# RWKV-7 projections on one Trainium2 core: TensorE in a written order, with tiles of their own for the keys' squares and the decay rows

## The chip, the cores and the metric

The kernel runs on one core of one Trainium2 chip. The metric is the time of one execution on the device, in microseconds (us); several executions are taken and their median stands for the kernel. A profile is one further execution, recorded instruction by instruction.

The engines are called by the names of the profile: PE (TensorE, matmuls), ACT (ScalarE), DVE (VectorE), POOL (GpSimd), and SP (SyncE), which in this kernel issues every data transfer (DMA).

## The reference, cut to what matters

The reference is an encoder trunk of two layers over 512 tokens of width 1024. Each layer is half an FFN, a token mixer, and half an FFN, with layer norms between them. The mixer of the first layer is neighbourhood attention, that of the second is RWKV-7. The change lies in the projections of the RWKV-7 mixer:

```python
xx = 0.5 * (x_prev + x_next) - x
xr, xw, xk, xv, xa, xg = (x + xx * mix[i] for i in range(6))
r = xr @ w_rkv[0];  k = xk @ w_rkv[1];  v = xv @ w_rkv[2]
wl = w0 + tanh(xw @ w1) @ w2            # for both directions z
decay = exp(-exp(-softplus(-wl) - 0.5))
a = sigmoid(a0 + (xa @ a1) @ a2)
g = sigmoid(xg @ g1) @ g2
kk = k * k_k;  kk = kk / max(norm(kk over each head's 64 channels), 1e-12)
```

A recurrent scan over the tokens in both directions follows; it reads all of these.

## The kernel before, in words

Everything is fp32. Where a product needs it, an operand is split into a high and a low part of a reduced type, by ACT (L220, the copy of the high part) and by DVE or POOL (L221, the difference), and a product takes three matmul passes (`mm3`, L225 to L227).

The kernel is written in a language that plans the order of the instructions itself. Its planner walks the program by an estimate of its own of how long everything takes, and puts onto each engine's queue the instruction that was traced earliest among those that are ready. A buffer of a tile pool is handed out when the first instruction that touches the tile is planned. On the chip each engine then runs its queue in that order. A block `manual_schedule(engines=...)` takes the engines named in it out of this: they get their instructions in the order of the program text. `behind(ins)` puts what is traced in its block behind `ins` on the engine of `ins`.

The stage in question is `rwkv_project` (from L570 on). On entry x lies as 8 chunks of 128 channels by 512 tokens (`xraw`). The stage works as follows, in the order of the text:

- `first(2)` (L607 to L623) makes `xx` and the split input `mk` of the keys, chunk by chunk; `mixed(i)` (L593 to L599) makes the split input of another projection: per chunk one DVE instruction at L603 into a tile of the tag `tmp`, one ACT copy (L220), one DVE difference (L221). `mw = mixed(1)` is the decay's input, `ma = mixed(4)` that of a, `mg = mixed(5)` that of the gate. `mg` takes the buffers of `mk`.
- The keys (L648 to L654): 8 input chunks by 8 output chunks into 8 PSUM banks `acc`. These are all the banks there are.
- `raws(3, dram["xv"])` (L631 to L637, called at L657) writes the values' unsplit input to DRAM: per chunk one DVE instruction (L635) into a `tmp` tile and one DMA of 256 KB. The values are computed in the scan, later.
- For each output chunk the bank is copied out by ACT (`store`, L626 to L629: an ACT copy into a quarter of one buffer `evs`, and a DMA), and its square goes by ACT (L661) into a `tmp` tile. A bank is free when both have read it. Eight products with the `heads` matrix (L664) sum the squares of each head into `ss`; two DVE instructions (L666, L667) invert them.
- The decay's first product `pw` (L670, weights w1) and its Tanh; a DMA brings the two halves of 64 rows to `tmp` tiles with a row of ones (L673 to L677), which are split into `wh`.
- `raws(0, dram["xr"])` and the product of its chunks with one column block of the receptance weights, `pr` (L679, L680).
- The product with a1 (L685), `mg`, the decay's second product (L687 to L698: 2 directions by 4 token blocks by 2 halves, each one `mm3`, an ACT Tanh at L696, a DVE instruction at L697 and a DMA), the gate's two first products (L705 to L707), its sigmoid (L711 to L713), and the gate's second product (L714 to L720).

The tag `tmp` has 4 buffers of 128x512. The larger buffers, of 128x2048, that hold `xx`, `evs`, `wh`, `gh`, `mw` and part of `ma` are of the tag `ring`, of which there are 11. Weights go through a `raw` tile and the tag `w`, of 3 buffers. A DMA, too, has its place in one queue, that of SP.

PE's order in this stage is the planner's.

Of the kernel before, what the change touches and what calls it, by code (L numbers as in the profile page):

```python
# [18 lines left out]
P = 128  # L19
# [79 lines left out]
class Trunk:  # L99
# [470 lines left out]
    def rwkv_project(self, dram, xraw, w_rkv, w1, w2, a1, g1, g2, heads):  # L570

        nc = self.nc
        with self.pool("rwa") as pool:
# [10 lines left out]
            evs, ev = quarters(), [0]  # L584
# [4 lines left out]
            def evac():  # L589
                ev[0] += 1  # L590
                return evs[:, ev[0] % 4, :]
# [39 lines left out]
            def raws(i, dst):  # L631

                for c in range(ND):
                    t = self.tmp()
                    nc.vector.scalar_tensor_tensor(t, xx[c], self.col(C_MIX + i, c), xraw[:, c, 1 : S + 1], ALU.mult, ALU.add)  # L635
                    nc.sync.dma_start(dst[:, c, :], t)
                    yield c, t  # L637
# [10 lines left out]
            acc = [self.bank() for _ in range(ND)]  # L648
            for c in range(ND):
                with self.behind(*marks):  # L650
                    u = k_units[c] if c < LEAD else self.load_rows(w_rkv[1], c * P)
                for o in range(ND):
                    self.mm3(halves_of(acc[o]), u[:, 0, o * P : (o + 1) * P], u[:, 1, o * P : (o + 1) * P],
                             *mk.get(c), c == 0, c == ND - 1)  # L654
            ma = mixed(4)

            list(raws(3, dram["xv"]))  # L657
            for o in range(ND):
                store(dram["rkv"][1][:, o, :], acc[o])
                sq = self.tmp()  # L660
                nc.scalar.activation(sq, acc[o], AF.Square, scale=self.col(C_KK, o))  # L661
                if o == 0:
                    ss = self.bank()[:HEADS]
                nc.tensor.matmul(ss, heads_t[:, o, :], sq, start=o == 0, stop=o == ND - 1)  # L664
            iv = evac()[:HEADS]
            nc.vector.tensor_scalar(iv, ss, 1e-24, None, ALU.max)  # L666
            nc.vector.reciprocal(iv, iv)  # L667
            nc.sync.dma_start(dram["iv"], iv)

            pw = self.proj_cols(self.load_cols(w1, 0), mw)  # L670
            wt = evac()
            nc.scalar.activation(wt, pw, AF.Tanh)
# [5 lines left out]
            pr = self.bank()  # L678
            for c, t in raws(0, dram["xr"]):  # L679
                nc.tensor.matmul(pr, wr[:, c, :], t, start=c == 0, stop=c == ND - 1)  # L680
            store(dram["rkv"][0][:, 0, :], pr)
            self.spares = None
            more.__exit__(None, None, None)

            store(dram["ah"], self.proj_cols(self.load_cols(a1, 0), ma))  # L685
            mg = mixed(5)
            for z in range(2):  # L687
                u = self.load_unit(w2[z])
                for t in range(NT):
                    for h in range(2):  # L690
                        pp = self.bank()
                        ws = slice(h * 512, h * 512 + 512)
                        ts = slice(t * P, t * P + P)
                        self.mm3(pp, *(wh[z][: CH + 1, i, ts] for i in range(2)), *(u[: CH + 1, i, ws] for i in range(2)), True, True)
                        th = evac()
                        nc.scalar.activation(th, pp, AF.Tanh, scale=0.5)  # L696
                        nc.vector.tensor_scalar(th, th, -0.5 * DECAY, -0.5 * DECAY, ALU.mult, ALU.add)  # L697
                        nc.sync.dma_start(dram["lw"][:, z, t, ws], th)  # L698

            u = self.load_cols(g1, 0)  # L700
            u2 = pool.tile([P, 2, ND, 32], F32R, name="g1b")
            raw = self.tmp()[:, : ND * 32].rearrange("p (c f) -> p c f", c=ND)
            nc.sync.dma_start(raw, g1[:, P:].rearrange("(c p) f -> p c f", p=P))
            self.split(u2[:, 0], u2[:, 1], raw)
            pg = [self.proj_cols(u, mg), self.bank()]  # L705
            for c in range(ND):
                self.mm3(halves_of(pg[1][:32, :]), u2[:, 0, c, :], u2[:, 1, c, :], *mg.get(c), c == 0, c == ND - 1)  # L707
            gn = (P, 32)
            for i, n in enumerate(gn):
                raw = self.tmp()[:n]  # L710
                nc.scalar.activation(raw, pg[i][:n], AF.Tanh, scale=0.5)  # L711
                nc.vector.tensor_scalar(raw, raw, 0.5, 0.5, ALU.mult, ALU.add)
                self.split(gh[i][:n, 0, :], gh[i][:n, 1, :], raw)  # L713
            ug = [self.load_rows(g2, 0), self.load_unit(g2[P:, :])]  # L714
            for c in range(ND):
                pp = self.bank()
                for i, n in enumerate(gn):
# [969 lines left out]
```

## Time and profile before

| what | value |
|---|---|
| time, median of 3 runs | 2276.62 us |
| lowest and highest of the runs | 2275.9 and 2277.72 us |
| the profiled execution: its time | 2277.85 us |
| the profiled execution: its span | 2276.0 us |
| PE busy, share of the span | 95% |
| mean granted TensorE clock | 0.979 |
| POOL, DVE, ACT busy | 63%, 48%, 43% |

Times inside a profile are counted from the start of its span. A row of the timeline gives start, duration, engine, line, operation, output and inputs, the number of merged instructions (x), and in brackets the idle time before it and what ended that. A row of the windows gives for a stretch its length, then for PE, weight loads, DVE, ACT and POOL the busy time and number of instructions, then the granted clock, the share of the DMA engines, and GB/s. A row of the groups gives busy time in total and the mean of one in ns, then the idle time before them. L220 and L221 are the lines of the split helper, L225 to L227 those of `mm3`, whoever calls them.

### The profile page before, as it was taken

The numbers are of one execution on the slowest core, as the hardware profiler recorded it, in microseconds if no ns is written. First come the engines' busy times: TensorE is split into PE (matmuls) and PEld (weight loads), VectorE is DVE, ScalarE is ACT, GpSimd is POOL, SyncE is SP. The second block draws the span as 40 slices with busy tenths as digits, with TensorE's granted clock in tenths as the row PEclk, the third lists the DMA queues.
The fourth block names the chain that finished last, engine by engine and source line by source line (L and its number), as shares of the span: only waits on it lengthen the run. The fifth ranks groups of instructions, "written<-read, shape, count | busy, mean of one in ns | idle before, by whom it ended". The sixth has DMA issues, their size and how long they took to land. (4 is left out here: it accounts for less than half of the span.)

```text
span 2276.0 us, 35138 instructions
## 1 busy us (share of the span) xinstructions
PE 2170.9 (95%) x13784; PEld 1709.4 (75%) x13784; DVE 1092.5 (48%) x1551; ACT 976.1 (43%) x1706; POOL 1423.2 (63%) x1235
## 2 busy tenths in 40 slices
PE   8999999999999999999999985799999998999998
PEld 7888878887888888788888773535666656888886
DVE  2333356276423333743333696435778636233336
ACT  3333335376333333533333434435777633333334
POOL 6878855554488886587877431224777722888763
PEclk9999999999999999999999997899999999999999
DMA  7444453432344445354444433674454642444443
GB/s 201 137 147 148 142 213 100 134 95 83 102 141 149 144 140 187 125 165 144 139 148 146 159 121 124 211 233 116 117 137 119 195 151 93 153 147 140 141 169 120
DMA packets 350497, 328.82 MB, mean 144 GB/s; under 512 B 48458, under 2 KB 277450, under 8 KB 350332
## 3 DMA queue, kind: packets, MB, share of 16 engines
q1 hardware_dynamic: 350332, 326.58, 45.4%
q8 instruction: 108, 1.77, 0.3%
q14 instruction: 57, 0.47, 0.1%
HBM read 262.26 MB, written 47.74 MB: 136 GB/s over the span
## 5 line engine op out<-in xcount | busy, mean ns | idle before, releaser
L221 POOL TENSOR_TENSOR w<-raw,w 128x1024 fp32r<-128x1024 f32 (+2 forms) x203 | 500.7, 2468 | 275.7 <-ACT w L220 257.6
L225 PE MATMUL bank<-xT,w 128*128 128x512 f32 x1416 | 552.5, 390 | 0.0
L226 PE MATMUL bank<-xT,w 128*128 128x512 f32 x1416 | 551.2, 389 | 0.1
L227 PE MATMUL bank<-xT,w 128*128 128x512 f32 x1416 | 551.0, 389 | 0.0
L220 ACT ACTIVATE w<-raw 128x1024 fp32r<-128x1024 f32 (+1 forms) x207 | 218.4, 1057 | 321.5 <-POOL ts L762 141.9
L422 DVE SCALAR_TENSOR_TENSOR ar<-bank,tmp 128x512 f32<-128x512 f32 x88 | 60.9, 691 | 581.3 <-PE bank L227 566.7
L227 PEld LDWEIGHTS bank<-xT,w 128*128 128x128 f32 x1416 | 265.8, 188 | 55.2
L226 PEld LDWEIGHTS bank<-xT,w 128*128 128x128 f32 x1416 | 265.9, 188 | 55.0 <-DVE xT L221 0.6
L225 PEld LDWEIGHTS bank<-xT,w 128*128 128x128 f32 x1416 | 265.9, 188 | 54.3 <-ACT ring L696 0.5
L791 PE MATMUL bank<-w,ring 128*128 128x512 f32 x864 | 201.5, 391 | 11.5 <-DVE w L221 10.3
L791 PEld LDWEIGHTS bank<-w,ring 128*128 128x128 f32 x864 | 161.5, 188 | 48.9 <-DVE w L221 13.3
L1354 POOL TENSOR_TENSOR tm<-qs,zs 128x126 f32<-128x126 f32 (+22 forms) x248 | 106.3, 429 | 133.4 <-DVE qs L1347 86.2
L791 PE MATMUL bank<-wx,an 128*128 128x512 f32 x792 | 187.3, 389 | 0.0
L791 PEld LDWEIGHTS bank<-wx,an 128*128 128x128 f32 x792 | 148.7, 188 | 30.8
L221 POOL TENSOR_TENSOR wx<-ra,wx 128x512 fp32r<-128x512 f32 x132 | 167.1, 1296 | 3.5 <-ACT wx L220 3.5
L221 DVE TENSOR_TENSOR ring<-ar,ring 128x1024 fp32r<-128x1024 f32 x44 | 133.1, 3025 | 74.5 <-ACT ring L220 74.4
L420 ACT ACTIVATE tmp<-bank 128x512 f32<-128x512 f32 x88 | 52.6, 598 | 232.1 <-PE bank L227 232.0
L221 POOL TENSOR_TENSOR ring<-raw,ring 128x1024 fp32r<-128x1024 f32 x28 | 69.7, 2500 | 100.4 <-ACT ring L220 100.4
L1356 POOL TENSOR_TENSOR zs<-zs,tm 128x126 f32<-128x126 f32 (+22 forms) x248 | 113.1, 456 | 19.4
L221 POOL TENSOR_TENSOR w<-late,w 128x1024 fp32r<-128x1024 f32 x28 | 71.7, 2563 | 75.6 <-ACT w L220 68.6
L220 ACT ACTIVATE wx<-ra 128x512 fp32r<-128x512 f32 x132 | 82.8, 633 | 72.0 <-PE bank L791 67.9
L225 PE MATMUL bank<-xT,ring 128*128 128x256 f32 (+1 forms) x352 | 103.6, 307 | 9.2 <-ACT xT L220 3.9
(283 smaller groups left out, 3736.2 us busy)
## 6 DMA issues: line engine op xcount, KB each, us to landing
raw<-in_ffn_w_in_dram SPq DMA_DIRECT2D x176, 512.0 KB, 3.7
ra<-in_ffn_w_out_dram SPq DMA_DIRECT2D x44, 1024.0 KB, 4.9
late<-d_late SPq DMA_DIRECT2D x30, 512.0 KB, 5.5
late<-in_ffn_w_out_dram SPq DMA_DIRECT2D x28, 512.0 KB, 4.4
raw<-in_w_qkv_dram SPq DMA_DIRECT2D x24, 512.0 KB, 3.8
d_late<-ts SPq DMA_DIRECT2D x44, 256.0 KB, 3.2
d_late<-ra SPq DMA_DIRECT2D x44, 256.0 KB, 2.0
xs<-ar SPq DMA_DIRECT2D x64, 128.0 KB, 2.3
```

Source lines behind the costliest of these rows:

```text
L220: self.hi = self.nc.scalar.activation(h, raw, AF.Copy).ins
L221: self.lo = (eng or self.nc.vector).tensor_tensor(l, raw, h.bitcast(F32), ALU.subtract).ins
L225: nc.tensor.matmul(out, wh, xh, start=start, stop=False)
L226: nc.tensor.matmul(out, wh, xl, start=False, stop=False)
L227: nc.tensor.matmul(out, wl, xh, start=False, stop=stop)
L420: nc.scalar.activation(s, pg, AF.Silu)
L422: nc.vector.scalar_tensor_tensor(raw[:, 3:7:3] if j else raw[:, 0:8:7], halves_of(pu), 0.5, halves_of(s), ALU.mult, ALU.mult)
L791: self.nc.tensor.matmul(acc, lhs, u[:, i], start=bool(first) and m == 0, stop=last and m == 2, skip_group_check=more)
L1354: nc.gpsimd.tensor_tensor(tv, qs[:, s, 0:s].rearrange("p (a o) -> p a o", o=1).broadcast_to([P, s, n]), zs[:, s : s + 1, c0:].broadcast_to ...
L1356: nc.gpsimd.tensor_tensor(zs[:, 0:s, c0:], zs[:, 0:s, c0:], tv, ALU.add)
```

## The change

PE gets its order from the text in the whole stage behind `mw`. Within it the text has a new order: keys; the keys' stores and squares; w1; a1; the sum of squares; the receptance block; the decay's direction 0; the gate's first products; the decay's direction 1; the values' input rows; the gate's second product. The squares get two `ring` tiles of their own, the decay rows lie in quarters of a second `evs` buffer (8 quarters are in turn from then on), the ones are set by POOL instead of DVE, and the split of the decay rows is queued on DVE behind the last of the receptance's 8 input rows. The number of matmuls, of transfers and of bytes stays the same.

```diff
-            evs, ev = quarters(), [0]
+            evs, ev = [quarters()], [0]
 def evac():
-                ev[0] += 1
-                return evs[:, ev[0] % 4, :]
+                ev[0] = (ev[0] + 1) % (4 * len(evs))
+                return evs[ev[0] // 4][:, ev[0] % 4, :]
 ...
             mw = mixed(1)
-            acc = [self.bank() for _ in range(ND)]
+            with self.tc.manual_schedule(engines=MANUAL):
+                acc = [self.bank() for _ in range(ND)]
 ...
-            ma = mixed(4)
-            list(raws(3, dram["xv"]))
-            for o in range(ND):
-                store(dram["rkv"][1][:, o, :], acc[o])
-                sq = self.tmp()
-                nc.scalar.activation(sq, acc[o], AF.Square, scale=self.col(C_KK, o))
-                if o == 0:
-                    ss = self.bank()[:HEADS]
-                nc.tensor.matmul(ss, heads_t[:, o, :], sq, start=o == 0, stop=o == ND - 1)
-            iv = evac()[:HEADS]
-...
-            for z in range(2):
-                raw = self.tmp()[: CH + 1]
-                nc.sync.dma_start(raw[0:CH], wt[z * CH : (z + 1) * CH])
-                nc.vector.memset(raw[CH:], 1.0)
-                self.split(wh[z][: CH + 1, 0, :], wh[z][: CH + 1, 1, :], raw)
+                sqs = [q[:, c, :] for q in (quarters(), quarters()) for c in range(4)]
+                for o in range(ND):
+                    store(dram["rkv"][1][:, o, :], acc[o])
+                    nc.scalar.activation(sqs[o], acc[o], AF.Square, scale=self.col(C_KK, o))
+                pw = self.proj_cols(self.load_cols(w1, 0), mw)
+                wt = evac()
+                nc.scalar.activation(wt, pw, AF.Tanh)
+                evs.append(quarters())
+                wts = [evac()[: CH + 1] for _ in range(2)]
+                for z in range(2):
+                    nc.gpsimd.memset(wts[z][CH:], 1.0)
+                    nc.sync.dma_start(wts[z][0:CH], wt[z * CH : (z + 1) * CH])
+                ma = mixed(4)
+                pa = self.proj_cols(self.load_cols(a1, 0), ma)
+                ss = self.bank()[:HEADS]
+                for o in range(ND):
+                    nc.tensor.matmul(ss, heads_t[:, o, :], sqs[o], start=o == 0, stop=o == ND - 1)
+                store(dram["ah"], pa)
+                iv = evac()[:HEADS]
+...
+                pr = self.bank()
+                for c, t in raws(0, dram["xr"]):
+                    nc.tensor.matmul(pr, wr[:, c, :], t, start=c == 0, stop=c == ND - 1)
+                with self.behind(self.lo, self.hi, self.mixed):
+                    for z in range(2):
+                        self.split(wh[z][: CH + 1, 0, :], wh[z][: CH + 1, 1, :], wts[z])
+...
+                mg = mixed(5)
+                decays(0)
+                u = self.load_cols(g1, 0)
+...
+                decays(1)
+                list(raws(3, dram["xv"]))
+                ug = [self.load_rows(g2, 0), self.load_unit(g2[P:, :])]
+...
```

`decays(z)` is the former loop over token blocks and halves for one z. `self.mixed` is the instruction that `raws` issued last on DVE (L635).

More of the change, by code (lines that the diff above doesn't have):

```diff
@@ L634, in raws @@
                     t = self.tmp()
-                    nc.vector.scalar_tensor_tensor(t, xx[c], self.col(C_MIX + i, c), xraw[:, c, 1 : S + 1], ALU.mult, ALU.add)
+                    self.mixed = nc.vector.scalar_tensor_tensor(t, xx[c], self.col(C_MIX + i, c), xraw[:, c, 1 : S + 1], ALU.mult, ALU.add).ins
                     nc.sync.dma_start(dst[:, c, :], t)
@@ L681, in rwkv_project @@
[L681 to L716, printed above, removed]
-                for i, n in enumerate(gn):
-                    cs = slice(c * P, c * P + P)
-                    self.mm3(pp, ug[i][:n, 0, cs], ug[i][:n, 1, cs], gh[i][:n, 0, :], gh[i][:n, 1, :], i == 0, i == 1)
-                store(dram["g"][:, c, :], pp)
+            with self.tc.manual_schedule(engines=MANUAL):
+                acc = [self.bank() for _ in range(ND)]
+                for c in range(ND):
+                    with self.behind(*marks):
+                        u = k_units[c] if c < LEAD else self.load_rows(w_rkv[1], c * P)
+                    for o in range(ND):
+                        self.mm3(halves_of(acc[o]), u[:, 0, o * P : (o + 1) * P], u[:, 1, o * P : (o + 1) * P],
+                                 *mk.get(c), c == 0, c == ND - 1)
+                sqs = [q[:, c, :] for q in (quarters(), quarters()) for c in range(4)]
+                for o in range(ND):
+                    store(dram["rkv"][1][:, o, :], acc[o])
[15 more added lines that the diff above has]
+                iv = evac()[:HEADS]
+                nc.vector.tensor_scalar(iv, ss, 1e-24, None, ALU.max)
+                nc.vector.reciprocal(iv, iv)
+                nc.sync.dma_start(dram["iv"], iv)
+                pr = self.bank()
[4 more added lines that the diff above has]
+                        self.split(wh[z][: CH + 1, 0, :], wh[z][: CH + 1, 1, :], wts[z])
+                store(dram["rkv"][0][:, 0, :], pr)
+                self.spares = None
+                more.__exit__(None, None, None)
+                def decays(z):
+                    u = self.load_unit(w2[z])
+                    for t in range(NT):
+                        for h in range(2):
+                            pp = self.bank()
+                            ws = slice(h * 512, h * 512 + 512)
+                            ts = slice(t * P, t * P + P)
+                            self.mm3(pp, *(wh[z][: CH + 1, i, ts] for i in range(2)), *(u[: CH + 1, i, ws] for i in range(2)), True, True)
+                            th = evac()
+                            nc.scalar.activation(th, pp, AF.Tanh, scale=0.5)
+                            nc.vector.tensor_scalar(th, th, -0.5 * DECAY, -0.5 * DECAY, ALU.mult, ALU.add)
+                            nc.sync.dma_start(dram["lw"][:, z, t, ws], th)
+                mg = mixed(5)
+                decays(0)
+                u = self.load_cols(g1, 0)
+                u2 = pool.tile([P, 2, ND, 32], F32R, name="g1b")
+                raw = self.tmp()[:, : ND * 32].rearrange("p (c f) -> p c f", c=ND)
+                nc.sync.dma_start(raw, g1[:, P:].rearrange("(c p) f -> p c f", p=P))
+                self.split(u2[:, 0], u2[:, 1], raw)
+                pg = [self.proj_cols(u, mg), self.bank()]
+                for c in range(ND):
+                    self.mm3(halves_of(pg[1][:32, :]), u2[:, 0, c, :], u2[:, 1, c, :], *mg.get(c), c == 0, c == ND - 1)
+                gn = (P, 32)
+                for i, n in enumerate(gn):
+                    raw = self.tmp()[:n]
+                    nc.scalar.activation(raw, pg[i][:n], AF.Tanh, scale=0.5)
+                    nc.vector.tensor_scalar(raw, raw, 0.5, 0.5, ALU.mult, ALU.add)
+                    self.split(gh[i][:n, 0, :], gh[i][:n, 1, :], raw)
+                decays(1)
+                list(raws(3, dram["xv"]))
+                ug = [self.load_rows(g2, 0), self.load_unit(g2[P:, :])]
+                for c in range(ND):
+                    pp = self.bank()
+                    for i, n in enumerate(gn):
+                        cs = slice(c * P, c * P + P)
+                        self.mm3(pp, ug[i][:n, 0, cs], ug[i][:n, 1, cs], gh[i][:n, 0, :], gh[i][:n, 1, :], i == 0, i == 1)
+                    store(dram["g"][:, c, :], pp)
```

14 lines of the change are left out of this document (removed).

## The prediction

> **What bounds the kernel now.** I read the page first: how busy PE is, and where it is not.
>
> ```profile
> PE 2170.9 (95%) x13784; PEld 1709.4 (75%) x13784; DVE 1092.5 (48%) x1551; ACT 976.1 (43%) x1706; POOL 1423.2 (63%) x1235
> ...
> PE   8999999999999999999999985799999998999998
> ...
> PEclk9999999999999999999999997899999999999999
> ```
>
> PE is the bound nearly everywhere. The one hole is in the 24th to 26th of 40 slices (digits 8, 5, 7), which is the stage of the projections. Then I read the windows and waits of that stage.
>
> ```profile
> 1374.00:1398.00 24.00, 0.26 (x1) 0.13 (x2) 17.71 (x22) 10.11 (x18) 5.29 (x2) 0.56 0.61 208
> ```
> ```profile
> PE bank L664 <- ACT tmp L661: 23.9, 1, 23.9
> ```
>
> PE stands still for 23.9 us, on ACT's first square. The timelines say what that square waited for, and what came first on each engine:
>
> ```profile
> 1351.96 0.39 PE L225 MATMUL bank<-xT,w 128*128 128x512 f32 x1
> ...
> 1373.50 0.39 PE L227 MATMUL bank<-xT,w 128*128 128x512 f32 x1
> ```
> ```profile
> 1380.63 0.63 ACT L220 ACTIVATE ring<-tmp 128x512 fp32r<-128x512 f32 x1 [2.06 <-DVE tmp L603]
> 1381.17 2.04 ACT L628 ACTIVATE ring<-bank 128x512 f32<-128x512 f32 x4
> 1383.10 0.63 ACT L220 ACTIVATE ring<-tmp 128x512 fp32r<-128x512 f32 x1
> ...
> 1397.00 1.28 ACT L661 ACTIVATE tmp<-bank,cols 128x512 f32<-128x512 f32 x2 [8.69 <-DMA d_xv<-tmp]
> ```
> ```profile
> 1383.59 2.06 DVE L635 SCALAR_TENSOR_TENSOR tmp<-ring,cols,xraw 128x512 f32<-128x512 f32 x3
> 1385.58 0.68 DVE L221 TENSOR_TENSOR ring<-tmp,ring 128x512 fp32r<-128x512 f32 x1
> 1386.29 4.70 DVE L635 SCALAR_TENSOR_TENSOR tmp<-ring,cols,xraw 128x512 f32<-128x512 f32 x4
> 1392.31 0.75 DVE L635 SCALAR_TENSOR_TENSOR tmp<-ring,cols,xraw 128x512 f32<-128x512 f32 x1 [1.31 <-DMA d_xv<-tmp]
> ```
>
> The keys end at 1373.50 + 0.39 = 1373.9. All eight banks are theirs, so PE can do nothing before ACT has stored and squared one. The stores come at 1381.17, behind the split of a's input, although the first bank was full before 1373.9. DVE ends that input at 1386.26; the values' rows begin among it and run until 1393.06, and their stores (d_xv) hold the four tmp tiles for which the square waits until 1397. Two causes are thus in series: ACT's place in its queue (to 1381) and the tmp tiles (to 1397).
>
> **The stretch that the sum is about** goes from 1373.9 to the end of the gate's last product.
>
> ```profile
> 1464.70 0.62 PE L227 MATMUL bank<-ring,w 32*128 32x512 f32 x1
> 1473.46 1.83 PE L1206 MATMUL a<-tri,lw 128*128 128x128 f32 x7 [8.14 <-DMA lw<-d_lw]
> ```
> ```profile
> 1405.02 2.75 PE L664 MATMUL bank<-tmp,heads 128*16 128x512 f32 x6
> ```
> ```profile
> 1430.42 1.88 PE L680 MATMUL bank<-tmp,wr 128*128 128x512 f32 x4
> ```
>
> It is 1465.3 - 1373.9 = 91.4 us long. A pass of `mm3` takes (1373.50 - 1351.96) / 95 = 0.227 us. Behind the keys come 24 + 24 (w1, a1), 48 (decay), 24 + 24 (gate, first), 48 (gate, second) = 192 passes, 43.6 us; 16 at L664 by 2.75 / 6 = 0.458, 7.3 us; 16 at L680 by 0.47, 7.5 us. The work is 58.4 us, so 33.0 us of the stretch are idle or slow. The change leaves the work and aims at these 33.0.
>
> **The change part by part.** The squares no longer take tmp tiles and the values' rows no longer stand in front of them, so the wait for d_xv is gone from this place. What is late next is ACT's place. The planner sets it, and the text in front of the keys' end is the same, so I expect ACT to reach the first store where it did, at 1381.17 behind the sixth or seventh chunk of a's input. Now its square follows at once:
>
> ```profile
> L661 ACT ACTIVATE tmp<-bank,cols 128x512 f32<-128x512 f32 x8 | 5.3, 688 | 14.0 <-DMA d_xv<-tmp 8.7 <-PE bank L664 5.2
> ```
>
> One bank is free at 1381.17 + 2.04 / 4 + 0.69 = 1382.4, with a signal 1382.6. **Term 1: a pause of 8.7 us**, between 0 (ACT takes the stores as the banks fill) and 11 (they come behind the last chunk of a's input, split at 1383.1 to 1383.7).
>
> ```profile
> 1378.00:1380.00 2.00, 0.00 (x0) 0.00 (x0) 2.00 (x1) 0.57 (x2) 2.00 (x1) 0.50 0.00 0
> 1398.00:1400.00 2.00, 2.00 (x3) 0.30 (x2) 0.00 (x0) 1.88 (x4) 0.00 (x0) 0.50 0.03 10
> 1400.00:1402.00 2.00, 2.00 (x6) 0.71 (x5) 0.00 (x0) 1.04 (x2) 0.00 (x0) 0.75 0.00 0
> ```
> ```profile
> 1397.74 3.49 PE L664 MATMUL bank<-tmp,heads 128*16 128x512 f32 x4 [23.85 <-ACT tmp L661]
> ```
>
> The granted clock (third last column) is at 0.50 from 1378 at the latest, 4 us into the pause, and comes back in the middle of the last stretch, at about 1401, 3.3 us after the restart. **Term 2: a restart at half clock, 1.7 us**; 0 if the pause stays well under 4 us.
>
> The w1 product then ends at 1382.6 + 1.7 + 5.4 = 1389.7, a1's at 1395.1 (its input is ready since 1386.3). Eight stores and squares are 8 x (0.51 + 0.69) = 9.6 us of ACT from 1381.2, with the splits and the Tanh between them some 13, so 1394: the sum of squares follows without a wait and ends at 1402.4. If the second tile of squares has to wait for a ring buffer, it gets one that w1's input leaves at 1389.7, and four more stores and squares end at 1394.5: no cost either.
>
> The receptance's first four rows are on DVE right behind a's input and lie ready. Rows 5 to 8 need the tmp tiles that PE frees, and DVE has the inverse of the norms in front of them:
>
> ```profile
> 1412.90 0.68 DVE L666 TENSOR_SCALAR ring<-bank 16x512 f32<-16x512 f32 x1 [0.18 <-PE bank L664]
> ```
> ```profile
> L667 DVE RECIPROCAL ring<-ring 16x512 f32<-16x512 f32 x1 | 3.3, 3334 | 0.0
> ...
> L221 DVE TENSOR_TENSOR ring<-tmp,ring 65x512 fp32r<-65x512 f32 x2 | 1.2, 642 | 0.0
> ```
>
> Clamp and reciprocal are 0.2 + 0.7 + 3.3 = 4.2 us, the row 0.75 (L603 below is the same instruction); PE has 4 x 0.94 = 3.8 us of rows in hand. **Term 3: 1.2 us**, 0 if row 5 gets ahead of the inverse. Row 5 is ready at 1407.3, row 8 at 1409.6, the two splits of the decay's rows behind it at 1410.9. The receptance ends at 1402.4 + 7.5 + 1.2 = 1411.1.
>
> Now the order is PE's own: direction 0 of the decay (5.4 us, to 1416.5; its split rows are just there), and then the gate, whose input `mg` needs the tmp tiles that the receptance held. DVE starts it at 1410.9:
>
> ```profile
> L696 ACT ACTIVATE ring<-bank 128x512 f32<-128x512 f32 x16 | 9.4, 593 | 12.8 <-DMA d_lw<-ring 8.8 <-PE bank L225 1.9 <-PE bank L227 1.4
> ...
> L697 DVE TENSOR_SCALAR ring<-ring 128x512 f32<-128x512 f32 x16 | 8.4, 543 | 6.1 <-ACT ring L696 6.1
> ...
> L221 DVE TENSOR_TENSOR xT<-tmp,xT 128x512 fp32r<-128x512 f32 x8 | 5.2, 682 | 0.1
> ```
> ```profile
> 1331.86 0.75 DVE L603 SCALAR_TENSOR_TENSOR tmp<-ring,cols,xraw 128x512 f32<-128x512 f32 x1
> 1332.53 0.69 DVE L611 TENSOR_TENSOR ring<-xraw 128x512 f32<-128x512 f32 x1
> ...
> 1334.64 2.78 DVE L603 SCALAR_TENSOR_TENSOR tmp<-ring,cols,xraw 128x512 f32<-128x512 f32 x1
> ...
> 1345.88 2.77 DVE L603 SCALAR_TENSOR_TENSOR tmp<-ring,cols,xraw 128x512 f32<-128x512 f32 x1
> ```
> ```profile
> 1334.31 5.37 POOL L221 TENSOR_TENSOR ring<-raw,ring 128x1024 fp32r<-128x1024 f32 x2 [5.21 <-ACT ring L220]
> 1339.64 8.47 POOL L221 TENSOR_TENSOR w<-raw,w 128x1024 fp32r<-128x1024 f32 x3
> ```
>
> Eight chunks by 0.75 + 0.68 are 11.4 us, eight decay instructions by 0.54 are 4.3. While POOL splits weights (five from 1334.31 to 1348.1) a DVE instruction of 0.75 us takes 2.78, so each such split beside it costs some 2 us; one falls here, that of the gate's second weights. 1410.9 + 11.4 + 4.3 + 2.0 = 1428.6, less 1.8 because successive instructions overlap by 0.08 (1331.86 + 0.75 against 1332.53; 23 times), plus 0.9 for the signal and the last chunk's three passes: 1427.7, where PE would have been through at 1416.5 + 5.4 = 1421.9. **Term 4: 6 us**, between 2 (decay instructions undisturbed, no split) and 10 (two splits). Before, the planner filled such waits with decay passes; a written order cannot.
>
> The other GpSimd edit, two memsets of one row, leaves DVE and lies on POOL long before the rows are needed. [...]
>
> The gate's sigmoid (Tanh, scaling, the two halves of a split: 0.6 + 0.5 + 0.6 + 0.7 us, the second one half beside the first) has direction 1 of the decay beside it, 5.4 us. **Term 5: 1 us**, because the values' rows now want the same tmp tiles; if they get them first, up to 11 (second rival).
>
> The values' rows with their eight DMAs move past the stores of the norms, the receptance and the decay on SP, to the end.
>
> ```profile
> 1482.40 7.01 SPq L1043 DMA_DIRECT2D xv<-d_xv x8
> ```
> ```profile
> d_xv<-tmp SPq DMA_DIRECT2D x8, 256.0 KB, 3.9
> ```
>
> Their reader comes 17 us after the gate's end; with 3.9 us to land they have to be late by 13 us to cost anything. I take 0, and 4 at most. The scan's start (8.14 us to its first matmul, for loads queued on SP behind the gate's stores) moves as a whole: 0, between -2 and 4.
>
> **Sum.** 8.7 + 1.7 + 1.2 + 6 + 1 = 18.6 us take the place of 33.0: 14.4 us less, 0.63%. The profiled execution took 2277.85 us (span 2276.0 and 1.85 around it), 1.23 over the median of the runs. 2277.85 - 14.4 = 2263.4, against the median 2262.2; I say 2262.
>
> As a check on term 4, the one unsure clock: an earlier wait of the same sort kept the clock.
>
> ```profile
> 1450.69 2.11 PE L225 MATMUL bank<-ring,w 128*128 128x512 f32 x8 [1.65 <-ACT ring L220]
> ```
>
> PE waited 1.65 us there and went on at 0.23 to 0.26 us per pass. Term 4 is cut into waits of about 0.8 us, one per chunk, so I add no slow restart. [...]
>
> **The rivals.**
>
> First, the pause closes altogether: ACT takes stores and squares as the banks fill. For it: they now stand in front of a's input in the text. Against: ACT's order before, in which seven chunks came first while nothing forced them to. Terms 1 and 2 go: 2262.2 - 10.4 = 2251.8.
>
> Second, the tmp tiles bite again at the gate. If the planner gives the values' rows the four tiles before the sigmoid, they take 1393.06 - 1383.59 = 9.5 us, as now, and the last one 3.9 to land, while the decay hides 5.4 and the chain is 3 us: PE waits 11 us more. 2273.
>
> Third, slower: PE's order is fixed, so all of `mg` lies bare behind the receptance, and POOL slows DVE throughout. Sixteen instructions at 2.8 us are 45 us in place of 11.4 + 2.0, so the gate comes 31 us later: 2293. It decides from about nine slow ones on (9 x 2.1 = 19 us to get from 2262 beyond 2281). For it: five in a row were slow from 1334.64 to 1348.65. Against: POOL has only the gate's second weights left to split then, unless all weights behind the receptance come late and in a bunch.
>
> Fourth, the change does not do what it says: the squares still wait, for a ring buffer that is in use until PE goes on. Then the pause stays at 24 us and the time where it was, 2276.6.
>
> **How the numbers follow.** My forecast has 0.60, the first rival 0.17, the second 0.11, the third 0.09, the fourth 0.03. About 0.2%, 4.6 us, is what can be told from no change. Faster: 0.60 + 0.17 = 0.77; the same: 0.11 (a part of it just faster or not) + 0.03 = 0.14; slower: 0.09. The range reaches down to the first rival with a little more from the scan's start, 2250, and up past the second, with a late scan's start, to 2276. The forecast's own bounds are 2252 to 2271.
>
> **What would show it.** In the profile after: PE's wait behind the keys, on ACT's square in place of d_xv, 5 to 11 us; the first store behind a's input on ACT; the gate's first product waiting for the difference at L221 in small pieces, 6 us in all; no slow DVE instruction but one or two; the values' rows behind `mg`; the gate ending some 15 us earlier, with the scan's first matmul still some 8 us behind it. I am wrong if ACT's stores come before 1376, if PE waits over 10 us for `mg` or the sigmoid, or if the scan's start grows.

## The result, and the profile after

The kernel after takes 2263.8 us (median of 5 runs, 2261.2 to 2266.3); the ratio to the kernel before is 0.9941, with a 95% interval of 0.9920 to 0.9962. The profiled execution took 2262.09 us, with a span of 2260.3.

The page of the profile after, in the lines that were shown of before: busy times, and the 40 slices of PE and of its clock.

```profile
PE 2169.9 (96%) x13784; PEld 1707.2 (76%) x13784; DVE 1084.6 (48%) x1549; ACT 974.6 (43%) x1706; POOL 1423.4 (63%) x1237
...
PE   8999999999999999999999988799999898999998
...
PEclk9999999999999999999999999899999999999999
```

The hole (8, 5, 7 before) is now 8, 8, 7. There is a new 8 further back, in slice 32. Both have to be read. The window of the stretch from the end of the keys to the end of the gate, first of before, then of after (length, then PE, weight loads, DVE, ACT, POOL; clock, DMA share, GB/s):

```profile
1373.89:1465.32 91.43, 65.20 (x224) 39.18 (x224) 53.35 (x73) 42.02 (x70) 20.98 (x10) 0.83 0.46 161
```
```profile
1369.69:1442.63 72.94, 65.26 (x224) 38.89 (x224) 48.64 (x69) 40.55 (x69) 22.12 (x13) 0.95 0.57 200
```

The same 224 matmuls take 18.5 us less (in the profile each of the eight products with `heads`, and of the eight of the receptance, counts as two). Of the difference of the two spans, 15.7 us, the other parts are: 4.2 less ahead of the stretch, where the two run the same matmuls in the same order, so this is how executions differ (after_again below, the same kernel as after, ends its keys 4.4 us later than after did); 0.7 less at the scan's start (8.14 to 7.49); 1.1 less in the scan up to the program's 11,000th matmul; 7.8 **more** in the next 200 matmuls (16.3 to 24.1); 0.9 more behind them. The waits of PE in the stretch after (total, times, longest; the first ends the stretch, at the scan's start):

```profile
PE a L1212 <- DMA mask<-in_smask_dram: 7.5, 1, 7.5
PE bank L225 <- ACT ring L659: 3.9, 1, 3.9
PE bank L226 <- DVE xT L221: 1.7, 2, 1.1
PE bank L681 <- DVE tmp L635: 1.1, 1, 1.1
PE bank L227 <- DVE g1b L221: 0.6, 1, 0.6
PE bank L225 <- ACT g1b L220: 0.4, 1, 0.4
```

The wait of 23.9 us on a square behind d_xv is gone. PE's wait on a square that is left is 3.9. ACT's timeline after tells why (the banks were full before 1369.7):

```profile
1370.94 0.63 ACT L220 ACTIVATE xm<-tmp 128x512 fp32r<-128x512 f32 x1 [2.55 <-DVE tmp L603]
1371.47 1.04 ACT L220 ACTIVATE w<-raw 128x1024 fp32r<-128x1024 f32 x1
1372.42 0.58 ACT L628 ACTIVATE ring<-bank 128x512 f32<-128x512 f32 x1
1372.90 0.68 ACT L659 ACTIVATE ring<-bank,cols 128x512 f32<-128x512 f32 x1
```

The first store stands behind the fourth chunk of a's input and a weight split. The new 8 in slice 32 is a wait of 5.8 us for one load of the output weights, `wv`:

```profile
PE a L982 <- DMA wv<-in_rw_out_dram: 5.8, 1, 5.8
```

SP's issues there, first of after, then of before:

```profile
1786.90 0.55 SPq L1484 DMA_DIRECT2D xs<-in_rw_out_dram  x1
1787.55 0.40 SPq L1482 DMA_DIRECT2D bk<-in_rw_out_dram  x1
1788.00 0.42 SPq L1484 DMA_DIRECT2D xs<-in_rw_out_dram  x1
1788.63 0.33 SPq L1473 DMA_DIRECT2D ar<-in_rw_out_dram  x1
1789.05 0.59 SPq L1473 DMA_DIRECT2D wv<-in_rw_out_dram  x1
```
```profile
1811.48 0.54 SPq L1476 DMA_DIRECT2D bk<-in_rw_out_dram  x1
1812.11 0.40 SPq L1467 DMA_DIRECT2D wv<-in_rw_out_dram  x1
1812.56 0.42 SPq L1478 DMA_DIRECT2D xs<-in_rw_out_dram  x1
```

The same loads, in another order: `wv`, which PE reads first, was second of five and is now last. Nothing of the diff is within 340 us of this place. The planner chose the order.

### The profile page after: what moved, and what is told of

It is laid out like the page before. It is cut to its first block, busy times and chain, and to the rows that moved or that the text cites. A ratio compares the mean times of both kernels' runs of the same rounds, so it can differ in the third digit from the quotient of the medians.

```text
span 2260.3 us, 35130 instructions
## 1 busy us (share of the span) xinstructions
PE 2169.9 (96%) x13784; PEld 1707.2 (76%) x13784; DVE 1084.6 (48%) x1549; ACT 974.6 (43%) x1706; POOL 1423.4 (63%) x1237
## 5 line engine op out<-in xcount | busy, mean ns | idle before, releaser
L221 POOL TENSOR_TENSOR w<-raw,w 128x1024 fp32r<-128x1024 f32 (+2 forms) x203 | 501.5, 2472 | 253.6 <-ACT w L220 240.1
L220 ACT ACTIVATE w<-raw 128x1024 fp32r<-128x1024 f32 x207 | 218.4, 1058 | 327.9 <-POOL ts L768 138.0
L221 POOL TENSOR_TENSOR wx<-ra,wx 128x512 fp32r<-128x512 f32 x132 | 166.8, 1291 | 3.5 <-ACT wx L220 2.4
L221 DVE TENSOR_TENSOR ring<-ar,ring 128x1024 fp32r<-128x1024 f32 x44 | 130.0, 2955 | 76.0 <-ACT ring L220 75.9
L221 POOL TENSOR_TENSOR ring<-raw,ring 128x1024 fp32r<-128x1024 f32 x28 | 69.7, 2499 | 105.6 <-ACT ring L220 105.6
L221 POOL TENSOR_TENSOR w<-late,w 128x1024 fp32r<-128x1024 f32 x28 | 71.3, 2547 | 75.9 <-ACT w L220 68.9
L220 ACT ACTIVATE wx<-ra 128x512 fp32r<-128x512 f32 x132 | 82.9, 633 | 72.4 <-PE bank L797 67.9
```

The lines of the kernel that those rows point to most:

```text
L220: self.hi = self.nc.scalar.activation(h, raw, AF.Copy).ins
L221: self.lo = (eng or self.nc.vector).tensor_tensor(l, raw, h.bitcast(F32), ALU.subtract).ins
```

## The experiments

Pause: PE's wait behind the keys. Stretch: end of the keys to end of the gate. Start: PE's wait at the scan's first matmul. wv: PE's wait for that load. All in us, from the profiled execution of each. The ratio is to the kernel before, run beside it.

| kernel | pause | stretch | start | wv | median us | ratio, 95% |
|---|---|---|---|---|---|---|
| before | 23.9 | 91.4 | 8.1 | 0.3 | 2276.6 | |
| after | 3.9 | 72.9 | 7.5 | 5.8 | 2263.8 | 0.9941 (0.9920 to 0.9962) |
| after_again | 4.1 | 73.1 | 7.7 | 5.2 | 2267.9 | 0.9949 (0.9936 to 0.9962) |
| tiles_only | 8.1 | 72.7 | 10.3 | 1.3 | 2261.5 | 0.9921 (0.9905 to 0.9937) |
| rows_last_only | 9.9 | 75.3 | 10.0 | 0.8 | 2263.0 | 0.9925 (0.9905 to 0.9944) |
| no_order | 4.4 | 74.8 | 9.8 | none | 2262.6 | 0.9930 (0.9911 to 0.9948) |
| wv_first | 4.4 | 72.9 | 8.1 | 1.6 | 2263.9 | 0.9931 (0.9916 to 0.9945) |
| stores_first | none | 71.8 | 7.8 | 5.1 | 2267.2 | 0.9940 (0.9920 to 0.9959) |
| gate_grouped | 4.1 | 72.0 | 9.3 | 6.0 | 2264.5 | 0.9936 (0.9915 to 0.9957) |
| both_decays | 4.1 | 79.3 | 8.2 | 0.5 | 2266.1 | 0.9941 (0.9925 to 0.9957) |
| all_edits | none | 74.7 | 9.5 | none | 2261.9 | 0.9922 (0.9909 to 0.9935) |
| quiet_pool | none | 67.9 | 8.1 | 5.7 | 2262.9 | 0.9926 (0.9912 to 0.9941) |
| last2 | none | 65.5 | 9.6 | none | 2250.1 | 0.9874 (0.9856 to 0.9892) |

The medians of the kernel before, run again beside the later kernels, were 2279.9 to 2281.1, so ratios compare better than times. Executions of one kernel differ by 2 to 13 us, and all intervals but the last overlap with that of the kernel after; differences among them are read from the stretch and the waits, of one execution each. "None" says that no row of the waits names it.

**Which part carries the gain?** Three kernels: the kernel before with one part, twice, and the kernel after without one.

```diff
 # tiles_only, against before
+            sqs = [q[:, c, :] for q in (quarters(), quarters()) for c in range(4)]
...
-                sq = self.tmp()
+                sq = sqs[o]
 # rows_last_only, against before: this line moves ahead of the gate's second product
-            list(raws(3, dram["xv"]))
...
+            list(raws(3, dram["xv"]))
             ug = [self.load_rows(g2, 0), self.load_unit(g2[P:, :])]
 # no_order, against after
-            with self.tc.manual_schedule(engines=MANUAL):
+            if True:
                 acc = [self.bank() for _ in range(ND)]
```

> The kernel before, with one edit: the eight squares of the keys get two ring buffers of their own and take no tmp tile. PE's order stays the planner's, the values' rows stay in front of the stores. Theory (two causes in series: the tmp tiles held PE from about 1381 to 1397 of the old pause, ACT's place in its queue the rest): no wait for d_xv is left on the squares, the pause behind the keys falls from 23.9 us to between 4 and 11, and about 13 us come off: 2264 us, 2260 to 2269. Rival (the place of the values' rows holds the pause, through DVE's and ACT's queues, whatever tiles the squares use): the pause stays over 18 us and the time at 2274 to 2279.

> The kernel before, with one edit: the values' input rows and their eight stores move from in front of the keys' stores to in front of the gate's second product. The squares keep the tmp tiles, PE's order stays the planner's. Theory (the tmp tiles were the trouble because the values' rows and their stores held them): with the rows gone the squares find tiles that the split of a's input leaves, so the pause falls to between 4 and 11 us here too, and the time to 2262 to 2270 us; what is late next is the tmp tiles at the sum of squares and the receptance. Rival (tmp tiles are short with or without these rows, because a's input, the squares and the receptance's rows need them too): the pause stays over 15 us and the time over 2271.

> The kernel after, with the written order of PE taken off: the same text, the squares' own tiles and the values' rows last, but PE's instructions of the stage in the planner's order again. Theory (the tiles and the rows' place carry the gain; the written order only trades waits for mg, some 4 us, against the planner's filling them): 2258 to 2266 us, the pause behind the keys within 3 us of 3.9. Rival (the written order carries the gain, because the planner puts the sum of squares straight behind the keys again and lets PE wait at its first square): a pause of over 8 us with the sum of squares next behind the keys, and 2268 to 2277 us.

PE behind the keys, in tiles_only's waits, then in rows_last_only's, then in no_order's:

```profile
PE bank L665 <- ACT ring L662: 8.1, 1, 8.1
```
```profile
PE bank L663 <- ACT tmp L660: 9.9, 1, 9.9
```
```profile
PE bank L225 <- ACT ring L659: 4.4, 1, 4.4
PE bank L226 <- DVE xT L221: 4.3, 3, 2.1
```

All three met the theory and none a rival. The squares' tiles alone or the rows' place alone removes the wait for d_xv, because either one breaks the chain "values' rows hold the tmp tiles that the squares need"; they do not add up. By ratio the whole change (0.9941) is no better than either of these two short edits (0.9921 and 0.9925). The written order on top of the other edits shortens the stretch by 1.9 us (74.8 to 72.9) and the start by 2.3 (less sure: gate_grouped, with the written order too, starts at 9.3); without it PE waits 4.3 us for mg rather than 1.7. But the kernel without it has its `wv` load second again and no wait there. The written order thus gives some 4 us up to the scan and loses 7 at its end, where the 200 matmuls take 17.0 us in no_order and 24.1 in after. The written order alone, on the kernel before, was not run.

**Is the loss at the scan's end the order of the loads?**

```diff
 # wv_first, against after (in outs)
-            nc.sync.dma_start(w[i], rows(self.w_out, i))
+            load = nc.sync.dma_start(w[i], rows(self.w_out, i)).ins
+            wv = wv if i else load
...
+                    with self.k.behind(wv):
                         nc.sync.dma_start(w[i], rows(self.w_out, i))
                         for c in range(EARLY, ND - 1):
                             nc.sync.dma_start(w[c], rows(self.w_out, c))
```

> The kernel after, with one edit far behind the stage: the last four loads of the output weights are queued on SP behind the load of wv, which PE needs first. Theory (the 7.8 us that the kernel after loses again near the end of the scan come from wv's load standing behind three others on the queues at 1786.9 to 1788.6): PE's wait of 5.8 us for wv goes, with the clock that fell to 0.50 behind it, and the time is 6 to 8 us less than the kernel after: 2256 us, 2253 to 2259. Rival (all transfers are full there, DMA share 1.00, so whichever load goes first the sum of them ends at the same time, and PE waits for a later one): the wait moves to another tile by about the same size and the time stays within 2 us of the kernel after, 2262 to 2266.

The wait fell from 5.8 to 1.6 us and the 200 matmuls from 24.1 to 19.9: 4.2 us of the 6 to 8 expected. SP issued the load no earlier than in after (7.6 us behind the 11,000th matmul, in after 7.3), but it landed 4.3 us after its issue in place of 8.6: fewer loads stood in front of it. In before it was issued at 5.9, so some wait was left here. The time did not show it: 2263.9, the rival's number, though the wait had not moved to another load. The other rows settle it. In all five rows whose SP queue has `wv` behind four other loads the wait is 5.1 to 6.0 us; in the eight where it is first or second it is 0 to 1.6. One of the five is the kernel after a second time:

> The kernel after, unchanged, on the chip and in the call of the next two kernels, so that their times stand beside it and its own stretch is seen twice. From the first profile: pause behind the keys 3.9 us, stretch from the end of the keys to the end of the gate 72.9 us, PE's wait for wv at the scan's end 5.8 us, ratio to the kernel before 0.992 to 0.996. If the wait for wv were chance and not the order of the loads, it would be under 2 us here.

So it is the order, and not chance.

**What is behind the pause, and is it worth closing?**

```diff
 # stores_first, against after
+                    first_sq = first_sq if o else sq      # sq: the square's instruction
...
-                ma = mixed(4)
+                with self.behind(first_sq):
+                    ma = mixed(4)
```

> The kernel after, with one edit: on ACT, the split of a's input is queued behind the first square of the keys. Theory (the pause of 3.94 us behind the keys is ACT's place in its queue: four chunks of a's input and a weight split stand in front of the first store, and the half clock of the w1 product, 3.05 us, follows from the pause): the first store comes before PE's last pass of the keys, the pause falls under 1 us, the w1 product takes 5.5 to 6 us at full clock, and the stretch from the end of the keys to the end of the gate falls from 72.9 us to 66 to 68. Rival (a's input, now later, takes the place of the squares): PE waits 3 us or more in front of a's product, the clock falls there instead, and the stretch stays within 2 us of 72.9. The time moves with the stretch: 2257 to 2259 us, or 2262 to 2266.

The pause closed and the w1 product took 5.6 us, but a's product then took 10.7 in place of 5.6. PE, DVE and POOL in stores_first at that place:

```profile
1382.93 0.51 PE L226 MATMUL bank<-ring,w 128*128 128x512 f32 x1 [2.38 <-DVE ring L221]
```
```profile
1379.37 0.75 DVE L635 SCALAR_TENSOR_TENSOR tmp<-ring,cols,xraw 128x512 f32<-128x512 f32 x1
1380.04 2.84 DVE L221 TENSOR_TENSOR ring<-tmp,ring 128x512 fp32r<-128x512 f32 x1
```
```profile
1379.55 2.77 POOL L221 TENSOR_TENSOR w<-raw,w 65x1024 fp32r<-65x1024 f32 x1 [7.65 <-ACT w L220]
```

The rival held: a's input is late. An instruction that takes 0.68 us takes 2.84 beside POOL's split of a weight, and rows of the receptance (L635) stand between a's chunks. ACT's place had hidden that DVE was nearly as late.

**The gate's second product, and the place of the decay.**

```diff
 # gate_grouped, against after
-                for c in range(ND):
-                    pp = self.bank()
+                for c0 in (0, 4):
+                    pps = [self.bank() for _ in range(4)]
                     for i, n in enumerate(gn):
+                        for c in range(c0, c0 + 4):
...
 # both_decays, against after
                 decays(0)
+                decays(1)
                 u = self.load_cols(g1, 0)
...
-                decays(1)
```

> The kernel after, with one edit: the gate's second product takes its passes of 128 rows for four banks together and then those of 32 rows for the same four, in place of three and three in turn. Theory (the 14.3 us of this product against 10.9 reckoned are 16 changes between 128 and 32 rows at some 0.21 us each): four changes are left, the product takes 11.6 to 12.2 us at full clock, and the stretch is 2.0 to 2.7 us shorter than 72.9. Rival (passes of 32 rows are slow in themselves, or the granted clock falls when 12 of them follow one another): the product takes 13.5 us or more, with passes of 32 rows at 0.3 us or a clock below 0.9 in its windows, and the stretch stays within 1 us of 72.9.

> The kernel after, with one edit: both directions of the decay stand in front of the gate's first product, where one stands in front of it and one behind. Theory (PE's waits for mg, about 2.5 us, are bare because only 6 us of decay cover DVE's 13 us of mg, and the sigmoid's 3 us are hidden only by the direction behind it): the waits for mg fall under 0.5 us, PE waits 2.5 to 4 us for the sigmoid in front of the gate's second product, and the stretch stays within 1.5 us of 72.9. Rival (DVE is the bound of this part: its decay instructions stand in the same queue as mg, so more of them in front make mg later): the waits for mg stay over 2 us, those for the sigmoid come on top, and the stretch is 76 us or longer. SP's loads of the output weights stand in this kernel as in the kernel before (wv second), so by the reading of the loss at the scan's end its wait for wv there is under 2 us.

In the kernel after, this product runs from 1428.32 to 1442.63, 14.3 us, all at a granted clock of 1.00. Its pattern, on PE's timeline of after:

```profile
1428.32 0.40 PE L225 MATMUL bank<-ring,w 128*128 128x512 f32 x1
1428.56 0.40 PE L226 MATMUL bank<-ring,w 128*128 128x512 f32 x1
1428.79 0.39 PE L227 MATMUL bank<-ring,w 128*128 128x512 f32 x1
1429.11 0.49 PE L225 MATMUL bank<-ring,w 32*128 32x512 f32 x1
1429.45 0.39 PE L226 MATMUL bank<-ring,w 32*128 32x512 f32 x1
1429.68 0.39 PE L227 MATMUL bank<-ring,w 32*128 32x512 f32 x1
1430.00 0.51 PE L225 MATMUL bank<-ring,w 128*128 128x512 f32 x1
```

Three passes take 14.3 / 16 = 0.89 us from change to change in place of 3 x 0.227 = 0.68: about 0.21 for each change of row count. Grouped by four, the product took 13.3 us: twelve passes of 128 rows 2.8 and of 32 rows 3.1, as the theory had it, but the next twelve of 128 rows took 4.4. The windows of gate_grouped show why (the clock is the third last column):

```profile
1436.00:1438.00 2.00, 2.00 (x10) 1.57 (x9) 0.18 (x1) 1.22 (x3) 1.04 (x2) 1.00 1.02 384
1438.00:1440.00 2.00, 2.00 (x6) 1.32 (x5) 0.00 (x0) 1.17 (x2) 0.00 (x0) 0.59 1.01 381
1440.00:1442.00 2.00, 2.00 (x6) 1.53 (x6) 0.00 (x0) 0.00 (x0) 0.00 (x0) 0.55 0.99 379
```

PE was busy throughout, and still the clock fell, at about 1438.4 by these means, behind twelve passes of 32 rows, which began at 1435.6. Both readings held a part. The kernel before shows the same, and could have shown it ahead of the prediction: there the planner put 23 of the 24 passes of 128 rows first, those of 32 rows began at 1456.13, and PE did not wait.

```profile
1458.00:1460.00 2.00, 2.00 (x9) 1.56 (x8) 0.00 (x0) 1.76 (x4) 0.00 (x0) 0.76 0.48 182
1460.00:1462.00 2.00, 2.00 (x7) 1.49 (x6) 0.00 (x0) 0.76 (x2) 0.00 (x0) 0.50 0.88 343
```

The clock fell at about 1459.0, 2.9 us into them, and the product took 14.6 us (1450.69 to 1465.32), no less than the alternating one of after.

In both_decays the waits for mg were gone and those for the sigmoid were 1.15 + 0.64 us, less than expected. But the stretch was 79.3, from neither reading: the gate's second product took 24.3 us, at half clock from 1434.3, 2.2 us behind the second of these waits, to its end, in the alternating pattern that ran at 1.00 in after:

```profile
1438.38 0.79 PE L225 MATMUL bank<-ring,w 32*128 32x512 f32 x1
1438.98 0.62 PE L226 MATMUL bank<-ring,w 32*128 32x512 f32 x1
1439.40 0.62 PE L227 MATMUL bank<-ring,w 32*128 32x512 f32 x1
```

**All together, twice.** all_edits joins stores_first, gate_grouped and wv's order and loads g1b ahead of the gate's input. quiet_pool and last2 follow from what it missed.

```diff
 # all_edits, besides the three: the four lines that load g1b move from behind decays(0) to here
+                u2 = pool.tile([P, 2, ND, 32], F32R, name="g1b")
...
                 mg = mixed(5)
 # quiet_pool, against stores_first
-                pw = self.proj_cols(self.load_cols(w1, 0), mw)
+                pw = self.proj_cols(self.load_cols(w1, 0, eng=nc.vector), mw)     # likewise a1 and w2[0]
...
+                m = self.mark(mg.get(ND - 1)[1].bitcast(F32)[:, 0, 0:1])
                 decays(0)
...
-                ug = [self.load_rows(g2, 0), self.load_unit(g2[P:, :])]
+                with self.behind(m):
+                    ug = [self.load_rows(g2, 0), self.load_unit(g2[P:, :])]
 # last2, against quiet_pool, besides groups of two banks and wv's order (a second `behind`
 # puts the late `ar` behind it too)
+                with self.behind(a_lo):                   # a_lo: DVE's last split of a's input
                     for c, t in raws(0, dram["xr"]):
```

> The kernel after, with four edits: the split of a's input behind the first square on ACT, the gate's second product in groups of four banks, the load of the last 32 columns of the gate's first weights (g1b) in front of the gate's input in the text, and the last four loads of the output weights queued behind wv's. Theory (the parts add up): pause and half clock 7.0, grouping 2.5, g1b 1.0 in the stretch, so 72.9 falls to 62 to 65 us, and 4 to 8 us at the end of the scan: 2247 to 2252 us. Rival (the scan's start is bound by the loads in front of it, so that PE waits longer for the mask or the decay rows by what the stretch gains): PE's wait at the scan's start grows from 7.5 us to 13 or more, and the time is 2256 to 2260.

> The kernel after, with three edits: the split of a's input behind the first square on ACT (as in stores_first); the second half of the splits of w1, a1 and the first decay weights on DVE in place of POOL; and POOL's splits of the gate's second weights behind the last chunk of mg. Theory (what bounds the stretch once the pause is closed is DVE, made slow by POOL's splits beside it: an instruction of 0.75 us takes 2.8): three splits cost DVE some 3 x 1.3 us but spare it 4 or 5 times 2.1 us, so PE's wait in front of a's product (3.2 us and a slow clock in stores_first, 71.8 us of stretch) falls under 1 us, that for mg from 1.7 to under 0.7, and the stretch is 65 to 68 us. Rival (DVE is the bound by its own work, and more splits on it only make it later): the waits stay over 3 us in all and the stretch is 71 to 75 us. SP's loads of the output weights stand as in the kernel after, so the wait for wv of about 5 us stays in either case: 2257 to 2260 us, or 2262 to 2267.

> The kernel quiet_pool with three edits more: the receptance's rows on DVE behind the last chunk of a's input; the gate's second product in groups of two banks (eight changes of row count for sixteen); the loads of the output weights queued wv first, as the kernel all_edits had them. Theory: the rows gave DVE 4 x 0.75 us among a's last chunks, so 1 to 2 us; eight changes at 0.21 us are 1.7; the stretch falls to 62 to 65 us with the granted clock at 1.00 through the gate, the wait for wv to under 1 us, and the time is 10 to 14 us below the kernel after of this call. Rival for the gate (six passes of 32 rows in a row are enough to bring the clock down, as twelve did): a clock of 0.5 to 0.7 in a window of the gate's second product and 13.3 us or more for it. Rival for the whole (the scan's start waits for its loads): PE's wait there grows from 7.5 to over 11 us and the time is within 6 us of the kernel after.

all_edits: the wait for wv went, but the stretch was 74.7, longer than after's. Neither reading held: the time was 2261.9, and the start 9.5 and not 13. The parts did not add up: PE waited 3.3 us in front of a's product, and 4.2 for mg, where one DVE instruction waited 0.9 us for a tmp tile (by the text, g1b had taken one) and another met POOL's split. Behind both waits the passes went at 0.43 us for a while in place of 0.227, and the grouped second product again lost its clock (0.50 from 1442 to 1444, 13.4 us). DVE, then POOL, in all_edits:

```profile
1414.82 2.85 DVE L603 SCALAR_TENSOR_TENSOR tmp<-ring,cols,xraw 128x512 f32<-128x512 f32 x1
```
```profile
1414.16 2.96 POOL L221 TENSOR_TENSOR w<-raw,w 128x1024 fp32r<-128x1024 f32 x1 [18.44 <-ACT w L220]
```

quiet_pool met the theory for the stretch (67.9) and for the wait for a's input (3.2 to 0.9), at the cost of splits that took 1.2 us each on DVE. One part of it missed: the waits for mg stayed at 1.7 us, with no POOL split beside mg at all. They are DVE's and ACT's own work, and not a split on POOL. Its time, 2262.9, is one that was named for the rival, but the kernel after took 2267.9 beside it: the median is 5.1 us lower, and the stretch is 5.2 us shorter.

last2 met the theory but for two sizes: the stretch was 65.5, and the time came out further down than the 10 to 14 us of the theory. There was no wait for wv, and the gate's second product took 12.7 us at a clock of 1.00 in groups of six passes. It beats both kernels: run side by side with after_again, 2250.1 against 2267.9. Of the 17.9 us between the two profiled spans 7.5 are the stretch, 7.8 the 200 matmuls at the scan's end (23.6 to 15.7), 3.4 lie ahead of the stretch, where both run the same matmuls and executions differ, 1.9 go back at the scan's start, and the rest of the scan and of the kernel makes up the last 1.1.

## Why the prediction came out right, step by step

The mechanism was right in the main. The tmp tiles held by the values' rows made the long wait, and with that wait gone ACT's place in its queue set the pause. But that the time came so close to 2262 is luck: the stretch became 4.1 us shorter than forecast (72.9 against 91.4 - 14.4 = 77.0), 7.8 us that had no term were lost at the scan's end, and the profiled execution was 4.2 us ahead before the stretch began. These three nearly cancel.

Of the prediction's own signs some failed. The pause of 3.9 us is below its 5 to 11, and ACT's first store came at 1372.42, before the 1376 that it named as a sign of being wrong. Part of that is the 4.2 us by which this execution was ahead: counted from the end of the keys, the store came 2.7 us behind it, where 1376 means 2.1 and the forecast 7.3. The gate ended 22.7 us earlier, and not some 15.

- **Term 1** was mis-sized: 3.9 us in place of 8.7. The step that failed is that ACT would reach the first store behind the sixth or seventh chunk of a's input, since the text ahead of it is the same. The planner now put it behind the fourth. What changed it is, as far as the runs show, the new order of the text behind the keys, in which a's input follows the stores: in no_order, with that text and no written order, the store comes behind the fourth chunk too and the pause is 4.4; in tiles_only and rows_last_only, where a's input still stands in front of the stores, it comes behind the seventh and the pause is 8.1 and 9.9. Where the planner puts an instruction could be bounded from the trace (0 to 11 was), not read from the old place.
- **Term 2** was too small: a pause of half the size still brought the clock down. The windows of after, 1372 to 1380:

```profile
1372.00:1374.00 2.00, 0.37 (x1) 0.37 (x2) 2.00 (x3) 2.00 (x5) 1.41 (x1) 0.68 0.05 22
1374.00:1376.00 2.00, 2.00 (x6) 1.52 (x6) 2.00 (x2) 2.00 (x5) 0.99 (x1) 0.50 0.62 241
1376.00:1378.00 2.00, 2.00 (x6) 1.58 (x5) 1.47 (x3) 2.00 (x5) 0.00 (x0) 0.50 0.74 170
1378.00:1380.00 2.00, 2.00 (x7) 1.57 (x6) 1.56 (x3) 2.00 (x5) 0.00 (x0) 0.61 1.09 388
```

  The w1 product took 8.5 us in place of 24 x 0.227 = 5.4: 3.1 us against 1.7. By the means of these windows the half clock set in at about 1372.7, 3 us into the pause, and lasted to about 1379.6, 6 us after PE went on. In before the half clock lasted 3.3 us after the restart, and the term was sized from that one restart.
- **Term 3** was right: 1.1 us against 1.2, the receptance's fifth row behind the inverse.
- **Term 4** was 4 us against 6: the gate's first products took 7.9 and 6.9 us in place of 5.4 each, with waits of 1.7 for mg and 1.0 for g1b. The DVE instructions for mg beside POOL's split ran at 0.67 to 0.73 us; POOL's split was the one that stretched, to 6.34. Of the 2 us that I set for one such collision, PE's waits show only what the difference for g1b paid (1.17 us, in all_edits 0.42). They are paid in full in no_order and all_edits (2.85 us). quiet_pool shows the 1.7 without any collision. That these waits add no slow restart was right: the clock stayed at 1.00 through the gate. In no_order and all_edits, with 4.3 and 4.2 us of waits for mg, there was one: behind the longest of them (2.1 and 2.7 us) the passes went at 0.43 us each in place of 0.227, the pace of the windows that show a clock of 0.50 (all_edits, 1442 to 1444), and the gate's first product took 13.2 and 12.8 us.
- **Term 5** was 0 against 1: the planner put the first half of the gate's sigmoid in front of the values' rows on DVE and the second behind three of them, and PE waited for neither.
- **No term** stood for the 16 changes of row count in the gate's second product, 14.3 - 10.9 = 3.4 us. I had reckoned it by passes at 0.227. In the kernel before there were few changes, but the clock fell and the product took 14.6 us: 3.7 of the 33.0 us "idle or slow" were lost there, and the sum dropped them and put nothing in their place.
- **The work** was reckoned a little high: the sum of squares and the receptance took 13.8 us without their wait, in place of 14.8.
- **The scan.** "Moves as a whole" was right at its start (7.5 against 8.1) and wrong at its end.
- **The rivals.** The first, that the pause closes by itself, did not occur; where an edit closed it (stores_first), 1.1 us came off the stretch, and not the 10.4 forecast or the 7.0 that pause and half clock cost here, since DVE was next. The second and the third did not occur. The fourth neither.

That the place of wv's load hangs on the written order is shown by no_order and after, which differ in nothing else. It is not the written order as such: both_decays has it too, with the decay in another place, and its load is second. Why the planner chose so was not tried.

## What to carry to other kernels

A wait with two causes in series is removed by breaking either one, so parts that each claim the whole gain must be timed alone: two here, of a few lines each, gave it singly, and all together gave no more. Behind a wait that is removed, look for the engine that is only a little less late (here DVE, slowed by POOL), and mend that before the next place in a queue. And where a planner orders the queues, compare the order of every queue after an edit, far from it too: PE waited 5 us more 350 us later, and two blocks of `behind` ended that.

## What the runs showed of the hardware

- PE needed about 0.21 us more at each change between passes of 128 and of 32 rows (after: 0.89 us from change to change in place of 0.68; with 16 changes the product took 14.3 us, with 8, in last2, 12.7).
- The granted clock fell to 0.5 with PE busy all the time, behind twelve or more passes of 32 rows in a row. Of the six kernels that have them the windows show it in five: 2.8 to 3.2 us behind the first of these passes in gate_grouped, before and all_edits, 4.1 in no_order, 5.3 in tiles_only. In the sixth, rows_last_only, the clock was still 1.00 from 1444 to 1446, and the last of these passes, 5.4 us behind the first, took 0.51 us in place of 0.38. (The last twelve of gate_grouped and all_edits ended, after 3.0 us, before the clock fell.) Six of them in turn with six of 128 rows kept 1.00 (last2, 12.7 us).
- Three and three in turn kept 1.00 in after (14.3 us), and kept 0.50 for 18 us in both_decays, where waits of 1.15 and 0.64 us stood ahead. So in these runs the pattern held the clock that it had; for the slow side this rests on one execution.
- Beside each other an instruction of DVE or one of POOL can take longer, and either can be the one. In stores_first a difference (L221) took 2.84 us on DVE beside a split of 2.77 on POOL, and 0.68 with none beside it; in all_edits a mixing (L603) took 2.85 beside a split of 2.96, and 0.74 a few us later with none. In after a split of some 2.4 us became 6.34 on POOL beside mg's instructions of 0.67 to 0.73 on DVE. The differences and the mixing have two inputs of 128x512. In quiet_pool a scaling with one input (L719) was stretched too, to 2.63 us beside a split, where the same in after (L716) took 0.41.
